# The last store of a 180-degree rotation, cut into five transfers

## The chip, the cores and the metric

The kernel runs on one core of one Trainium2 chip. The metric is the time of one execution on the device in microseconds (us); lower is better. The time before is 122.03 us, the median of three runs (121.81 to 122.38).

## The reference

```python
def setup_inputs():
    batch, c, h, w = 32, 3, 256, 256
    return {"x": np.random.randn(batch, c, h, w).astype(np.float32)}

def reference(x):
    return np.rot90(x, k=2, axes=(-2, -1)).astype(np.float32)
```

Each of the 96 images of 256 x 256 float32 values is turned by 180 degrees. Seen as one line of 65,536 values, an image comes out in reverse order. 25.17 MB are read and 25.17 MB written; there is no arithmetic.

## The kernel before

The 96 images are cut into three groups of G = 32. An image is cut into four rows of E = 16,384 values (64 KiB), so that a group fills a tile of 128 partitions with 64 KiB in each: partition 4n + s holds quarter s of image n. The three groups have tiles of their own, A, Bt and Ct; a smaller tile T of 2,048 values a partition serves as a buffer.

The work has three steps for each tile:

- **Load.** `load` (L56) brings A and Bt in one transfer each. Ct comes in three, through `rows` (L72): the even partitions, then partitions 1, 5, 9 and so on, then 3, 7, 11 and so on.
- **Turn in place.** `turn` calls `swap`, which reverses each partition's row: a piece from the back is copied reversed into T, the matching piece from the front is copied reversed to the back, and T is copied to the front. All copies are on VectorE and have the line L44. A and Ct are turned in 4 pieces of 2,048 columns, Bt in 6 of up to 1,366. The first piece of a tile takes in the first and the last columns, the last piece the middle ones. The copies keep the order in which they are written.
- **Store.** `store` (L59) writes a tile in one transfer; `[:, ::-1]` on the output's side puts quarter s in the place of quarter 3 - s, which completes the reversal of the image.

All DMAs, loads and stores, are issued by SP on one queue. The first store is tied by hand to the last copy of Bt, and the last copy but one of Bt to the second load of Ct (`after`), so that stores start when the loads are nearly in. The last store follows when Ct has been turned. Line L122 is the end of the program, where SP waits for all transfers and then for the other engines.

Of the kernel before, what the change touches and what calls it, by code (L numbers as in the profile page):

```python
# [2 lines left out]

os.environ.setdefault("NEURON_RT_ULTRASERVER_MODE", "4")

# [4 lines left out]


@with_exitstack
def kernel(
    ctx: ExitStack,
    tc: tile.TileContext,
    x: bass.AP,
    out: bass.AP,
):
    nc = tc.nc  # L20
    P = 128

    B, C, H, W = x.shape
    L = H * W
    G = 32
    E = L // 4
    J = E // 8

    x4 = x.rearrange("b c h w -> (b c) (h w)").rearrange(
        "(g n) (s e) -> g (n s) e", n=G, s=4)  # L30
    o4 = out.rearrange("b c h w -> (b c) (h w)").rearrange(
        "(g n) (s e) -> g n s e", n=G, s=4)

    pool = ctx.enter_context(tc.tile_pool(name="slots", bufs=1))
    A = pool.tile([P, E], x.dtype, tag="A")
    Bt = pool.tile([P, E], x.dtype, tag="B")
    Ct = pool.tile([P, E], x.dtype, tag="C")
    T = pool.tile([P, J], x.dtype, tag="T")

    def back(t, lo, hi):  # L40
        return t[:, hi - 1:(lo - 1 if lo else None):-1]

    def copy(dst, src):
        c = nc.vector.tensor_copy(out=dst, in_=src)  # L44
        tc.keep_in_program_order(c)
        return c

    def after(later, earlier, why):
        tc.add_manual_dep(
            later.ins, earlier.ins.name,  # L50
            mybir.DependencyInfo(
                mybir.DependencyClass.Sync, mybir.DependencyReason.DATA),
            reason=why)

    def load(t, g, lo, hi):
        return nc.sync.dma_start(out=t[:, lo:hi], in_=x4[g][:, lo:hi])  # L56

    def store(t, g, lo, hi):
        return nc.sync.dma_start(  # L59
            out=o4[g][:, ::-1, lo:hi], in_=t[:, lo:hi])  # L60

    def swap(t, lo, w):
        hi = E - lo - w
        return [
            copy(T[:, 0:w], back(t, hi, hi + w)),
            copy(t[:, hi:hi + w], back(t, lo, lo + w)),
            copy(t[:, lo:lo + w], T[:, 0:w])]

    half = E // 2

    def rows(first, step):
        return nc.sync.dma_start(  # L72
            out=Ct[first::step, :], in_=x4[2][first::step, :])

    load(A, 0, 0, E)
    load(Bt, 1, 0, E)
    rows(0, 2)
    ahead = rows(1, 4)
    rows(3, 4)

    def turn(t, pieces):
        done = []
        step = -(-half // pieces)
        for lo in range(0, half, step):
            done += swap(t, lo, min(step, half - lo))
        return done

    turn(A, 4)
    *_, last_but_one, last = turn(Bt, 6)
    after(last_but_one, ahead,  # L90
          "this copy starts when all loads but two rows are in")
    first = store(A, 0, 0, E)
    after(first, last, "the first store goes two copies after that")
    store(Bt, 1, 0, E)
    turn(Ct, 4)
    store(Ct, 2, 0, E)


# [1 line left out]
_INS = ['x']  # L100
_OUTS = [((32, 3, 256, 256), 'float32')]


# [23 lines left out]
```

## Time and profile before

| what | value |
|---|---|
| median of three runs | 122.03 us (121.81 to 122.38) |
| the profiled execution's own time | 122.06 us |
| its span, first to last instruction | 120.3 us |
| VectorE busy | 45.2 us (38%), 42 copies |
| the data queue's packets, as a share of 16 DMA engines | 97.3% |
| bytes moved, mean rate over the span | 50.33 MB, 418 GB/s |
| issue to landing: A, Bt (loads) | 22.0 us, 40.9 us |
| issue to landing: A, Bt, Ct (stores) | 22.3 us, 40.9 us, 42.7 us |
| granted TensorE clock | 1.00 (TensorE is not used) |

A page of the profile tells the busy time of each engine, the DMA queues with their packets, who waited for whom, and each DMA's time from issue to landing. A transfer is cut into packets, which 16 DMA engines carry; behind the data of a transfer each engine that served it sends a packet of 4 bytes, the completion, which counts up a semaphore. The trace holds start, duration and size of each packet, but not the number of the DMA engine that carried it. An engine can be followed through the trace since its next packet starts 3 to 4 ns before the end of the one ahead.

### The profile page before, as it was taken

How to read it: one execution, taken by the hardware profiler on the slowest of the kernel's cores; microseconds unless marked ns; L12 is line 12 of the kernel's file. 1: busy time of each engine (PE TensorE's matmuls, PEld its weight loads, DVE VectorE, ACT ScalarE, POOL GpSimd, SP SyncE). 2: the span in 40 equal slices, each digit the busy share in tenths (PEclk: the TensorE clock that was granted, in tenths of full speed). 3: DMA queues.
4: the chain of work that ended last, by engine and by line, in shares of the span. 5: the costliest groups of instructions: out<-in, count | busy, mean ns of one | idle time of the engine just before them, and what ended most of it. 6: DMA issues, size and time to landing. Idle time of an engine off the chain costs nothing.

```text
span 120.3 us, 101 instructions
## 1 busy us (share of the span) xinstructions
DVE 45.2 (38%) x42; POOL 0.2 (0%) x4
## 2 busy tenths in 40 slices
DVE  0000000499995099999459999400000000000000
POOL 0000000000000000000000000000000000000000
DMA  9889998899889988998899889988998889888980
GB/s 349 349 349 392 588 414 349 371 610 414 349 349 610 436 349 349 567 479 349 349 501 545 349 349 414 632 349 349 392 654 349 349 349 697 349 349 349 676 371 0
DMA packets 897, 50.33 MB, mean 418 GB/s; under 512 B 129, under 2 KB 129, under 8 KB 129
## 3 DMA queue, kind: packets, MB, share of 16 engines
q1 hardware_dynamic: 896, 50.33, 97.3%
q14 instruction: 1, 0.00, 0.0%
HBM read 25.17 MB, written 25.17 MB: 418 GB/s over the span
## 4 chain that ended last, share of the span: by engine, by line
DMA 34%; DVE 26%; another core or an unknown queue 2%; issue 1%; SPq 0%; DVEq 0%
DMA Bt<-in_x_dram 34%; DVE Bt L44 9%; DVE T L44 9%; DVE Ct L44 8%; SPq L56 0%; DVEq L44 0%
## 5 line engine op out<-in xcount | busy, mean ns | idle before, releaser
L44 DVE COPY T<-A 128x2048 f32<-128x2048 f32 x4 | 4.9, 1227 | 22.9 <-DMA A<-in_x_dram 22.8
L44 DVE COPY T<-Bt 128x1366 f32<-128x1366 f32 (+1 forms) x6 | 5.2, 874 | 4.5 <-DMA Bt<-in_x_dram 4.3
L44 DVE COPY T<-Ct 128x2048 f32<-128x2048 f32 x4 | 4.9, 1227 | 3.2 <-DMA Ct<-in_x_dram 3.1
L44 DVE COPY Bt<-T 128x1366 f32<-128x1366 f32 (+1 forms) x6 | 5.2, 872 | 0.2
L44 DVE COPY Bt<-Bt 128x1366 f32<-128x1366 f32 (+1 forms) x6 | 5.2, 872 | 0.2
L44 DVE COPY Ct<-T 128x2048 f32<-128x2048 f32 x4 | 4.9, 1227 | 0.1
L44 DVE COPY A<-A 128x2048 f32<-128x2048 f32 x4 | 4.9, 1227 | 0.1
L44 DVE COPY A<-T 128x2048 f32<-128x2048 f32 x4 | 4.9, 1227 | 0.1
L44 DVE COPY Ct<-Ct 128x2048 f32<-128x2048 f32 x4 | 4.9, 1227 | 0.1
L111 POOL MEMSET const-bfloat16-1.0<- 128x1 bf16 x1 | 0.1, 101 | 0.0
L111 POOL MEMSET const-uint8-127<- 128x1 uint8 x1 | 0.1, 101 | 0.0
L111 POOL MEMSET const-float32-0.0<- 128x1 f32 x1 | 0.1, 98 | 0.2 <-issue 0.2
L111 POOL MEMSET const-float32-1.0<- 128x1 f32 x1 | 0.1, 98 | 0.0
## 6 DMA issues: line engine op xcount, KB each, us to landing
Ct<-in_x_dram SPq DMA_DIRECT2D x3, 54.4
A<-in_x_dram SPq DMA_DIRECT2D x1, 22.0
Bt<-in_x_dram SPq DMA_DIRECT2D x1, 40.9
out_dram<-A SPq DMA_DIRECT2D x1, 22.3
out_dram<-Bt SPq DMA_DIRECT2D x1, 40.9
out_dram<-Ct SPq DMA_DIRECT2D x1, 42.7
```

Source lines behind the costliest of these rows:

```text
L44: c = nc.vector.tensor_copy(out=dst, in_=src)
L111: nc = _bacc.Bacc("TRN2", target_bir_lowering=False, num_devices=1)
```

## The change

The last store, of tile Ct, is issued as five transfers in place of one:

1. of the partitions 3, 7, 11 and so on (the output's quarter 0 of each image), the first 320 columns (1,280 B) for images 0 to 24: 25 rows,
2. the same for images 25 to 31: 7 rows,
3. all even partitions, full rows: 64 rows,
4. the partitions 1, 5, 9 and so on, full rows: 32 rows,
5. the partitions 3, 7, 11 and so on, columns 320 to 16,383: 32 rows of 64,256 B.

Loads, copies, and the stores of A and Bt stay as they are.

```diff
+    def store_split(t, g, w):
+        n = 0
+        for k in (25, 7):
+            nc.sync.dma_start(
+                out=o4[g][n:n + k, 0, 0:w],
+                in_=t[4 * n + 3:4 * (n + k):4, 0:w])
+            n += k
+        nc.sync.dma_start(out=o4[g][:, 3::-2, :], in_=t[0::2, :])
+        nc.sync.dma_start(out=o4[g][:, 2, :], in_=t[1::4, :])
+        nc.sync.dma_start(out=o4[g][:, 0, w:E], in_=t[3::4, w:E])
+
...
     turn(Ct, 4)
-    store(Ct, 2, 0, E)
+    store_split(Ct, 2, 320)
```

## The prediction

> **What bounds the kernel now.** I read the page first (busy shares, then the DMA part), then the DMA queue's waits, then the last stretch in windows, then the single packets.
>
> ```profile
> DVE 45.2 (38%) x42; POOL 0.2 (0%) x4
> ...
> DMA packets 897, 50.33 MB, mean 418 GB/s; under 512 B 129, under 2 KB 129, under 8 KB 129
> ...
> q1 hardware_dynamic: 896, 50.33, 97.3%
> ```
>
> VectorE works 38% of the span; the 16 DMA engines together are busy 97.3% of it. The queue's 896 packets are 768 of 65,536 B, 48 for each engine, and 128 of 4 B, the completions of 8 transfers on 16 engines. A big packet takes 2.42 us (27.1 GB/s), and on each engine one starts 3 to 4 ns before the end of the one ahead. The first starts at 1.74 us and the last ends at 119.12, so between these two nothing but DMA bytes per engine sets the time.
>
> ```profile
> SPq L59 <- DVE Bt L44: 35.7, 1, 35.7
> SPq L122 <- DMA out_dram<-Ct: 19.3, 1, 19.3
> SPq L59 <- DMA A<-in_x_dram: 19.3, 1, 19.3
> SPq L122 <- DMA out_dram<-Bt: 19.3, 1, 19.3
> SPq L59 <- DVE Ct L44: 15.2, 1, 15.2
> ```
>
> These are waits of SP, the engine that issues every DMA. The line at L59 for Ct (15.2) ends when the last copy of Ct is done, at 76.7 us. The store then issued queues behind store Bt, whose completions start at 99.5. That is 22 us of cover: VectorE and the issue are not on the path. The last wait (L122, Ct, 19.3) ends at 119.48 with the landing of the last store. From there to the end of the span, 0.80 us, is closing work.
>
> ```profile
> 116.00:116.25 0.25, 0.00 (x0) 0.00 (x0) 1.00 1.21 524
> 116.25:116.50 0.25, 0.00 (x0) 0.00 (x0) 1.00 4.24 1835
> 116.50:116.75 0.25, 0.00 (x0) 0.00 (x0) 1.00 4.24 1835
> 116.75:119.13 2.38, 0.00 (x0) 0.00 (x0) 1.00 0.00 0
> ```
>
> The last column is GB/s, put down where a packet starts: 524 in 0.25 us is 2 packets of 65,536 B, 1835 is 7. So the 16 last packets start spread out, and end from 118.59 to 119.12, with a mean of 118.88. The kernel ends with the latest engine, and perfect levelling could give 0.24 us. Packet by packet, the five engines that begin the first load earliest (1.74 to 1.81) are the five that end earliest (118.59 to 118.81); the sixth and seventh to begin end at 118.84 and 119.07, and the latest of the other nine at 119.12.
>
> **The change, part by part.**
>
> *Bytes per engine.* The last store writes the same bytes. Its last transfer (32 rows, two for each engine) is shorter by 1,280 B a row: each engine sheds 2,560 B, at 2.42 us for 65,536 B that is 0.095 us. The 32 pieces come back as transfers of 25 and 7 rows. No row of the trace shows a transfer whose rows do not divide by 16. All those in it (128, 64, 32 rows) gave every engine that served them equally many rows; if that holds, 25 rows go to five engines, five each (or to one), and 7 rows to seven engines, one each (or to one). I take five and seven, and the engines that begin first, since the split has a use only then; both are open, and are rivals below. So engines 1 to 5 get six pieces, 6 and 7 one, the other nine none.
>
> *A piece of 1,280 B.* By bytes it is 0.047 us. The smallest data-queue packet, the 4-byte one, shows 9 ns, so with it 0.056 us: the low end. The high end comes from the nearest odd rows, the 8,192 B instruction packets on the other queue: 0.32 to 0.53 us where bytes make 0.30, so up to 0.23 us above bytes, 0.28 us a piece. I take 0.056: the store packets stand back to back, as these pieces will, while those instruction packets stood alone before the span. Below bytes it cannot come; the big packets show no faster rate.
>
> *Completions.* Store Ct goes from one transfer to five. Engines 1 to 5 get four more 4-byte packets, 6 and 7 three, the others two. From the end of one big packet to the start of the next is -3 ns without a completion and +2 to +3 ns with one: 6 ns each, 0.024, 0.018 and 0.012 us.
>
> *End of the data.* Engines 1 to 5: 118.81 - 0.095 + 6 x 0.056 + 0.024 = 119.08. Engines 6 and 7: 119.07 - 0.095 + 0.056 + 0.018 = 119.05. The other nine: 119.12 - 0.095 + 0.012 = 119.04. Latest 119.08 against 119.12: a gain of 0.04 us.
>
> *Order of the rows.* The even rows, then every fourth, in place of all 128. Loads of Ct already go in this pattern and land 9.67, 4.85 and 4.84 us apart, 19.36 together; the load of Bt took 19.35. Store packets now average 2.423 us and load packets 2.420. By the pattern I cost nothing; were the eight last packets as quick or slow as the extremes of the steady rows (2.418 and 2.432), it would be -0.04 or +0.07 us.
>
> *Issues and waits.* The program as built lets the 25-row transfer wait for the third copy of Ct only, since that copy writes the columns 0 to 319 last. So SP issues 25 and 7 rows at about 65.4 us, and then waits for the last copy, as now. The even rows go out at 76.7 and the last two after them, 0.54 to 0.60 us each (rows L59 and L72), done by 78.6. The queue works in order on each engine (landings now come strictly in order of issue), so nothing moves before 99.5, and the cover is 21 us; without it four more issues would cost 2.4 us. Behind SP's new waits stand only its own later stores. No engine waits for the first two.
>
> *The closing waits.* The built program keeps eight completion counters. With 12 transfers in place of 8, four counters are used twice, and the last transfer lands on that of the second Ct load. SP's four closing waits test two counters each, in an order that does not change, and that counter is in the first. Now three of them pass before the last store lands (at 77.3, 80.8 and 100.1) and only the fourth waits for it; after the change the first waits for it, and the other three, long satisfied, stand behind it. In the trace one such wait, from its start to the next instruction, is 119.482 to 119.550, 0.068 us. Three: +0.20 us, with no cover. From below: nothing, if satisfied waits pass at once; from above, three times the 0.1 us that separate some of the barrier's steps behind.
>
> **Sum.** -0.04 + 0.20 = +0.16 us on the profiled execution, which had a span of 120.28 and a time of 122.06 (1.78 outside the span, unchanged): 122.22. The median of the three runs shown is 0.03 below it, so 122.2. This is +0.13%; a measurement of this kernel can tell about 0.5%, 0.61 us, from no change.
>
> **Rivals.**
> *Dear pieces (slower).* Place: engines 1 to 5, behind store Bt, at about 99.5 us. A piece at 0.28 us makes 118.81 - 0.095 + 6 x 0.28 + 0.024 = 120.42, 1.30 later, with the closing waits 123.56. It decides over 0.5% from 0.13 us a piece (119.53 = 118.74 + 6 x 0.13). For it: the first packet of each engine, at 2.86 to 3.65 us, shows what work outside a stream can cost. Against: the 3 ns overlap of neighbours. Chance 0.11.
> *All on one engine.* 32 x 0.056 = 1.79 us on a single engine, ending 1.19 to 1.72 us later: 123.5 to 124.0. Rows of the trace neither exclude nor show it. Chance 0.03.
> The Trainium skill (DMA: Bandwidth & Descriptors, section on why a DMA increments its semaphore by 16) says that the engines used are the largest number up to 16 that divides both sides' slowest dimension, the lowest-numbered first: 25 rows on five, 7 on seven. By that rule this rival falls and the sum stands; no row here can show it.
> *Each transfer pays its landing.* If an engine held back until a transfer's completion had landed (118.59 to 118.96 now for the first: 0.37 us), four more would cost engines 1 to 5 1.5 us, less the 0.3 by which they were early, with the closing waits: 123.4. Against it: on each engine the next transfer's first packet starts 3 ns before the completion packet ends, with no gap. Chance 0.03.
> The same page (section on the anatomy of one DMA) gives each transfer a fixed 2.0 us, most of it waiting for the receipt; four more, one behind the other, would make 130 us. The trace disagrees, as the three loads of Ct show with 19.36 us.
> *The early engines are not those served (the change does not do what it says).* If the latest of all is among the five: 119.12 - 0.095 + 0.336 + 0.024 = 119.39, with the waits +0.47: 122.5. Chance 0.13; a third of that, with pieces a little dearer, passes 0.5%.
> *Closing waits free.* -0.04: 122.0, chance 0.10.
> *Faster by over 0.5%.* Even perfect levelling is 0.24 us; only a faster packet rate would do it, and none of the 768 is below 2.418 us. Chance 0.03.
>
> **How the numbers follow.** Forecast 0.57; with free waits and two thirds of the unserved case, within 0.5%: 0.57 + 0.10 + 0.09 = 0.76. Slower: 0.11 + 0.03 + 0.03 + 0.04 = 0.21. Faster 0.03. The range goes from 121.85 (free waits, the quick rows' -0.04, 0.1 of spread between medians) to 122.95 (a piece of about 0.18 us), leaving out some 0.15 above and 0.04 below.
>
> **What would show it.** Right: 12 x 16 - 20 = 172 completions of 4 B and 32 packets of 1,280 B; their duration near 0.056 us; last data end near 119.08; four closing waits close together after the last landing, and 1.0 us instead of 0.80 from the landing to the end. Wrong: pieces of over 0.13 us, 25 of them on one chain, gaps behind completions, or a steady packet off 2.42 us.

## The result, and the profile after

The changed kernel takes 122.47 us (median of 7 runs, 122.43 to 122.69), the kernel before 122.01 (7 runs, 121.81 to 122.38). The ratio is 1.0039 with a 95% interval of 1.0026 to 1.0053: about 0.46 us slower (0.32 to 0.65), inside the range of the forecast (122.2, from 121.85 to 122.95) and within the 0.5% that was called no change. The changed kernel's profiled execution took 122.46 us, with a span of 120.67.

From the page after, the same three lines as were read before:

```profile
DVE 45.2 (37%) x42; POOL 0.2 (0%) x4
...
DMA packets 972, 50.33 MB, mean 417 GB/s; under 512 B 172, under 2 KB 204, under 8 KB 204
...
q1 hardware_dynamic: 972, 50.33, 97.1%
```

172 completions, and 204 - 172 = 32 packets under 2 KB, the pieces: as forecast. The other 768 are 736 of 65,536 B and 32 of 64,256 B. VectorE has not moved. SP's waits (engine, line, what it waited for, us in all, times, longest):

```profile
SPq L133 <- DMA out_dram<-Ct: 39.7, 1, 39.7
...
SPq L69 <- DVE Ct L44: 9.1, 1, 9.1
SPq L65 <- DVE Ct L44: 3.9, 1, 3.9
```

The two small transfers go out after a wait on VectorE of 3.9 us at L65, the even rows after another 9.1 us at L69: these two stand in place of the 15.2 us of before. At the end there is one wait of 39.7 us, where before the waits for stores A, Bt and Ct came one after the other: the first closing wait now holds the last store's counter. The trace has it from 80.037 to 119.699 us, and behind it three more at 119.741, 119.808 and 119.873.

The windows over the last packets of the changed kernel (last column: GB/s of the packets that start in the stretch):

```profile
116.00:116.25 0.25, 0.00 (x0) 0.00 (x0) 1.00 0.59 257
116.25:116.50 0.25, 0.00 (x0) 0.00 (x0) 1.00 3.56 1542
116.50:116.75 0.25, 0.00 (x0) 0.00 (x0) 1.00 4.16 1799
116.75:117.00 0.25, 0.00 (x0) 0.00 (x0) 1.00 1.19 514
```

At 64,256 B a packet these are 1, 6, 7 and 2. Before, none started after 116.75. The spread between engines has grown, not shrunk.

The 0.40 us between the two profiled executions have two parts. The last data are the end of the last packet of rows; a landing is the last step of a completion counter.

| execution | last data of store Bt | last data of all | from the one to the other | last landing | from it to the span's end |
|---|---|---|---|---|---|
| before | 99.757 | 119.124 | 19.367 | 119.466 | 0.81 |
| after | 99.742 | 119.350 | 19.608 | 119.677 | 0.99 |

0.18 us are closing work, and 0.24 us are data behind store Bt. (Store Bt ended 0.015 us earlier in the execution after, and the landing came 0.015 us closer behind the data, which is why the two add up to slightly more than 0.40.)

### The profile page after: what moved, and what is told of

It reads as the page before. It is cut to its first block, busy times and chain, and to the rows that moved or that the text cites. A ratio compares the mean times of both kernels' runs of the same rounds, so it can differ in the third digit from the quotient of the medians.

```text
span 120.7 us, 105 instructions
## 1 busy us (share of the span) xinstructions
DVE 45.2 (37%) x42; POOL 0.2 (0%) x4
## 4 chain that ended last, share of the span: by engine, by line
DMA 34%; DVE 25%; another core or an unknown queue 2%; issue 1%; SPq 0%; DVEq 0%
DMA Bt<-in_x_dram 34%; DVE Bt L44 9%; DVE T L44 9%; DVE Ct L44 8%; SPq L56 0%; DVEq L44 0%
```

## The experiments

All times are against the kernel before on the same chip and day. Differences are of medians; ratios and their intervals are of means, so the two need not agree in the last digit. Two columns of the table above are given with most runs, since they are free of what happened ahead of the last store: "end" is the time from the last landing to the span's end, "data" the time from the last data of store Bt to the last data of all. One profiled execution stands behind each of these. In the six profiles with equal bytes for each engine or with pieces of 256 B, "data" lies between 19.31 and 19.41.

**1. The closing waits alone, and the pieces alone.** Stores A and Bt are cut into four and two transfers, all of rows that divide by 16. That moves the last store's counter into the first closing wait of the kernel before (12 transfers), and into the last one of the changed kernel (16).

```diff
-    first = store(A, 0, 0, E)
+    def quarter(t, g, s):
+        return nc.sync.dma_start(out=o4[g][:, 3 - s, :], in_=t[s::4, :])
+
+    first = quarter(A, 0, 0)
...
-    store(Bt, 1, 0, E)
+    for s in (1, 2, 3):
+        quarter(A, 0, s)
+    nc.sync.dma_start(out=o4[1][:, 3::-2, :], in_=Bt[0::2, :])
+    nc.sync.dma_start(out=o4[1][:, 2::-2, :], in_=Bt[1::2, :])
```

> The kernel before, with store A as four transfers of 32 rows and store Bt as two of 64: 12 transfers, so that the last store's counter falls in the first of SP's four closing waits, as in the changed kernel; the last store itself is one transfer of 128 rows. Theory (closing waits cost 0.20 us, the pieces on the five served engines cost the rest): +0.20 us against before, four closing waits together after the last landing, the last data end where it was (119.12 give or take 0.1). Rival (the closing waits only look dear, the time is in the data): within 0.05 us of before.

Measured +0.14 us (1.0013, interval 1.0005 to 1.0022). From the last landing to the span's end 0.99 us, the data behind store Bt 19.373. The closing wait stands out in the waits of this kernel:

```profile
SPq L128 <- DMA out_dram<-Ct: 42.2, 1, 42.2
```

> The changed kernel with the same cut of stores A and Bt: 16 transfers, the last store's counter falls in the last closing wait again. Theory: 0.20 us below the changed kernel, about +0.25 us against before, since the pieces stay. Rival (all of the loss is closing work): equal to before.

Measured +0.29 us (1.0020, 1.0009 to 1.0030): end 0.82 us again, data 19.558. SP's closing wait falls apart into four again, as before the change:

```profile
SPq L139 <- DMA out_dram<-Ct: 39.4, 4, 20.4
```

The theory holds in both: the closing waits and the data are separate prices, 0.14 and 0.29, and their sum, 0.43, is the change's 0.46 but for the measurement's width.

**2. Light pieces.** `store_split(Ct, 2, 64)`, with 12 transfers and then with 16.

> The changed kernel with pieces of 64 columns (256 B) in place of 320. Theory (the five served engines are not the early ones, and their load sets the end): a piece is about 0.018 us, the served engines gain 0.11 + 0.02 - 0.02 us in place of 0.27, so the end comes some 0.15 us sooner than in the changed kernel: +0.3 us against before. Rival (the odd transfers cost by their number, whatever they carry): as the changed kernel, +0.46. Rival (the forecast's: the served engines are early, the others set the end and are now relieved less): 0.08 us later than the changed kernel, +0.54.

Measured +0.21 us (1.0017, 1.0009 to 1.0026): end 1.00, data 19.382. Both rivals are out; the theory's +0.3 lies at the upper end of the interval (0.11 to 0.32 us). Of 32 pieces 31 show 0.018 us. The pieces label the engines here: the five that carry six of them ended store Bt at 99.360, 99.408, 99.442, 99.507 and 99.565, places 2, 4, 6, 8 (or 9, two end together) and 11 of 16 in order of ending. The latest (99.800) was none of them.

> Pieces of 256 B and 16 transfers: both prices taken away at once, the five transfers of the last store kept. If closing waits and the load of the served engines are all, it equals before within 0.1 us; if five transfers cost something else, it stays 0.15 us or more above.

Measured +0.01 us (1.0001, 0.9992 to 1.0010): 121.96 against 121.95. With both prices taken away the five transfers cost nothing, and bring nothing either. This shows that the price in the data goes with the bytes of the pieces on the engines they serve; it does not tell how.

**3. Five transfers without odd rows.** First with transfers that take images 0 to 15 and 16 to 31 apart:

```diff
+    def store_split(t, g, w):
+        for n in (0, 16):
+            nc.sync.dma_start(
+                out=o4[g][n:n + 16, 3::-2, :], in_=t[4 * n:4 * n + 64:2, :])
+        nc.sync.dma_start(out=o4[g][:, 2, :], in_=t[1::4, :])
+        for n in (0, 16):
+            nc.sync.dma_start(
+                out=o4[g][n:n + 16, 0, :], in_=t[4 * n + 3:4 * n + 64:4, :])
...
-    store(Ct, 2, 0, E)
+    store_split(Ct, 2, 320)
```

> The last store in five transfers whose rows all divide by 16 (even rows of images 0 to 15 and 16 to 31, then partitions 1, 5, 9 and so on, then 3, 7, 11 and so on for images 0 to 15 and 16 to 31): each engine gets the same eight packets of 65,536 B as before. Theory: closing waits alone, +0.20 us, data end moved by no more than the completions' 0.02. Rival (cutting the store or its row order costs in the data): +0.4 us or more.

Measured 136.21 us, +14.29 (ratio 1.1173, 1.1148 to 1.1197). Neither theory had this. The transfer of 32 rows over all partitions took its usual time (123.0 to 124.9 us at the landings, behind 120.0); the others, whose 16 engines all read from one half of the partitions, took about twice theirs: the second landed 10.3 us behind the first. Two kernels tell cutting from halves apart: one with a transfer for each quarter of the image over all partitions and the last quarter in two halves of its columns, and one that only cuts the last store of the kernel before into partitions 0 to 63 and 64 to 127.

> The last store in five transfers of 32 rows over all 128 partitions (one for each quarter, the last quarter in two halves of its columns): no odd piece, equal bytes for each engine, 12 transfers. Theory (closing waits cost 0.13 to 0.20 us, cutting by itself nothing; the 14 us of the five equal transfers came from reading 64 of the 128 partitions): +0.15 to +0.20 us. Rival (cutting the store in five costs by itself): +10 us or more, as there.

Measured +0.18 us (1.0016, 1.0004 to 1.0027): end 0.99, data 19.383. Five transfers cost their closing waits and nothing else.

> The kernel before with its last store in two transfers, partitions 0 to 63 and 64 to 127: full rows, 64 rows each, nine transfers. Theory (16 engines that read the same 64 partitions get about half their rate: in the five equal transfers 32 rows from one half took 9 to 10 us where 4.84 is usual): the last store takes up to twice its 19.35 us, +15 to +19 us. Rival (it was the small number of rows or the strides there): within 0.1 us of before.

Measured 142.61 us, the median of two runs, +20.64 (1.1692, 1.1670 to 1.1715). The windows show it, with store Bt in the first line and the two halves in the others:

```profile
82.00:98.00 16.00, 0.00 (x0) 0.00 (x0) 1.00 1.07 459
102.00:118.00 16.00, 0.00 (x0) 0.00 (x0) 1.00 0.95 197
122.00:136.00 14.00, 0.00 (x0) 0.00 (x0) 1.00 1.04 220
```

The column before the last is the busy share of the DMA engines: they are as busy, at half the bytes (459 GB/s, then 197 and 220). The longest packets took 5.3 us. One thing stays open: in both slow kernels a transfer from half of the partitions also writes only half of the group's images, one half of its 8.39 MB of output. No run has the one without the other, so that it is argued, but not shown, that reading from half of the partitions is the cause.

**4. Where the odd transfers lose their time.** In the changed kernel's packet records 27 of the 32 pieces took 0.055 us, and five took 0.095, 0.099, 0.120, 0.168 and 0.224. Followed along the engines, two of the five served engines (those with six pieces) needed about 0.55 and 0.70 us for them and their completions, the other three 0.32 to 0.39. (The two and an engine without pieces end store Bt within 3 ns, so that it is not certain which is which.) One of the two also stood idle for 0.22 us between two pieces, from 99.513 to 99.732. That made two theories: A, the hold-ups; and B, the plain load of an engine that is late already. First the pieces on all engines, in one transfer:

```diff
-        for k in (25, 7):
-            ...
+        nc.sync.dma_start(out=o4[g][:, 0, 0:w], in_=t[3::4, 0:w])
```

> The 32 pieces of 1,280 B go in one transfer of 32 rows in place of 25 and 7, so all 16 engines get two pieces each, from the partitions of which they also carry the full rows; 11 transfers, so two closing waits stand behind the last landing. Theory (in the changed kernel two of the five served engines were held up for 0.2 to 0.4 us at their pieces, since these come from partitions that other engines are reading at the time): no piece much over 0.055 us, data end moved by +0.02, closing +0.13: +0.15 us against before. Rival (a piece is dear wherever it comes from, 0.1 us and more): +0.25 us or more. Rival (the load of the five engines alone, without hold-ups, makes the loss): +0.15 us, but then pieces_last stays at +0.46.

Measured +0.17 us (1.0008, 0.9998 to 1.0019): end 0.93 (two waits behind), data 19.414. All 32 pieces took 0.055 us. Two on each of 16 engines are not dear. Then the two small transfers behind the large ones:

> The changed kernel with the 25 and 7 rows issued behind the three large transfers; the same packets for each engine, 12 transfers, three closing waits behind the last landing. Theory (hold-ups from partitions that others read): the early engines' pieces run beside the others' last full packets, the late ones' alone, so hold-ups shrink where they count: +0.25 to +0.40 us against before. Rival (the load of the five engines alone): the same bytes on the same engines, +0.46 us as in the changed kernel.

Measured +0.57 us (1.0046, 1.0031 to 1.0060), where the theory of hold-ups forecast 0.25 to 0.40, which only touches the lower end of the interval (0.38 to 0.73). No piece was held up, all took 0.055 us, and the time stayed. Once more, with a second profile:

> The changed kernel with the 25 and 7 rows last, once more, for a second profile: the pieces were 0.055 us each without a hold-up, and the time was +0.56. Theory B: from the last landing of store Bt to the last landing of all some 0.1 to 0.2 us more than the 19.36 us of before, time +0.35 to +0.5. Rival (a small transfer at the end lands later behind its data, 0.4 to 0.56 us where full rows take 0.35): the same data end as theory B, and 0.1 to 0.2 us on top, +0.5 to +0.6.

Measured +0.53 us (1.0045, 1.0032 to 1.0057). In the two profiles the data behind store Bt took 19.300 and 19.258 us, 0.07 and 0.11 *less* than before: here the levelling works. But the last landing came 0.55 and 0.45 us behind the last completion packet, 0.34 in the kernel before, and the end cost 0.99 us. These make +0.32 and +0.18; in both profiles store Bt ended late, too, at 99.90 and 99.96. Whether that is chance stays open, and with it 0.25 to 0.35 us of this kernel. So its time is no proof for theory B: it stayed, but not by way of the data.

The changed kernel once more:

> The changed kernel once more, for a second profile. Theory A (held-up pieces): again two or more of the five served engines are held up for 0.2 us and more at their pieces, and one of these ends last. Theory B (the five served engines stand anywhere in the order, and 0.33 us of pieces on a late one sets the end): the five engines hold places spread over the sixteen by the end of store Bt, and the last to end is a served one, held up or not. Time +0.46 us in both.

Measured +0.54 us (1.0042, 1.0030 to 1.0054): end 1.00, data 19.576. One served engine was clearly held up (0.221 and 0.098 us for two pieces), but it was the one that had ended store Bt first of all, at 99.198, so it cost nothing. The last to end was a served engine without a hold-up: it ended store Bt at 99.782, 2 ns before the latest of all, and began its next full row at 100.126, 0.344 later. The profile of after_16_transfers says the same: the latest of all at the end of store Bt (99.983) was a served one, and began its next row 0.324 later. Theory B holds in these two. In the first profile of the changed kernel theory A does: the last to end was one of the two held up, from place 6, 7 or 8, while the five served engines stood early, at places 1, 3, 10 and two of 6 to 8. Then three times the bytes:

> The changed kernel with pieces of 960 columns (3,840 B). Theory B: a piece takes about 0.146 us in place of 0.052, six of them 0.56 us more, while each engine sheds 0.19 us more in the last rows: +0.37 us on the changed kernel, +0.83 against before. Theory A (hold-ups, which come with each odd piece and not with its bytes): +0.27 us or less above the changed kernel's data end less 0.19, so +0.3 to +0.5 against before. The forecast's picture (served engines early by 0.3 us): +0.5.

Measured +1.88 us (1.0132, 1.0104 to 1.0160, or 1.27 to 1.95 us), more than any theory said. Theory A's bound and the forecast's picture are out, and B's +0.83 falls short as well. The profiled run does not help: it took 122.64 us, the fastest of six (123.43 to 123.89 the others); in it 31 of 32 pieces took 0.149 us, and the five served engines stood at place 7 or before. What happens in the others was not seen; that hold-ups grow with the bytes is a guess.

## Why the prediction was right, and where it was not

**The closing waits: right.** Forecast +0.20 us for three satisfied waits behind the last landing; 0.18 in the profile, +0.14 and +0.18 as times (12 transfers with nothing else changed, and five even transfers). It follows from the completion counters, as the built program shows them, and undoing that alone gives it back.

**Issues, cover, order of rows, completions: right.** SP issued 25 and 7 rows at 65.2 and 66.1 us and the rest from 76.6. Here the issues were dearer than the 0.54 to 0.60 us taken: five took 0.87, 1.26, 0.60, 1.38 and 1.36 us. The last is done at 80.0 in place of 78.6, against 99.3, when the first engine has ended store Bt (99.2 in the kernel before, where the forecast wrote 99.5); the cover holds. Rows by quarters cost nothing (five even transfers: data 19.383 against 19.367).

**Five and seven engines: right.** The counters tell it: that of the 25 rows rose at once at 66.45 us and then in five landings from 99.88 to 100.40, that of the 7 rows in seven. Here is the row that the forecast lacked for the rule of the Trainium skill (DMA: Bandwidth & Descriptors, section on why a DMA increments its semaphore by 16) by which 25 rows go to five engines and 7 rows to seven, and it agrees. That those are the lowest-numbered engines the trace cannot show.

**Which engines, and what six pieces cost them: wrong.** The step that failed is the end of the data. It let the five served engines end store Bt first, 0.3 us ahead of the latest, gave each 0.36 us for six pieces and their completions, and came out at -0.04 us; measured is +0.24. The two halves of that step failed in different executions.

In the profile of the changed kernel the places were nearly as forecast: the last of the five to end store Bt did so at 99.512, 0.23 us ahead of the latest engine. The latest engine that was not held up ended 19.343 us behind store Bt, 0.02 less than before. What failed there is the price: two of the five took 0.55 and 0.70 us in place of 0.36, and the slower one ended last.

In the profiles of after_16_transfers and changed_again the places failed: a served engine ended store Bt last of all, or 2 ns from it. On an engine that is late already the sum of the forecast gives 0.27 us more, and 6 x 0.052 + 0.02 - 0.095 = 0.24 with the pieces' measured spacing; these two profiles have 0.19 and 0.21. This is the rival "the early engines are not those served", 122.5 with a chance of 0.13. That its figure was met so closely is in part luck, since the first profile has its 0.24 by the other road. The range of the forecast held because it was wide enough for this rival; of the two terms of its sum, -0.04 and +0.20, only the second came.

The forecast took five early engines out of one profile and put the five served ones in their place, with the reason that the split has a use only then. In the five profiles in which the served engines can be told, they lean to the early side: 23 of their 25 places are among the first eleven of 16. But the forecast needed all five early in every execution, and one late one is enough to set the end. In the profile before, moreover, the link from the first to begin to the first to end leads through 60.3 to 60.9 us, between the last load and the first store. There about ten engines pause for 0.03 to 0.13 us, and none of these can be followed with certainty.

**A piece: right in most, with a tail.** Forecast as 0.056 us, it took 0.055, 27 times of 32; the other five took up to 0.224. The dear pieces of the rival (0.28 for each) did not come, the worst engine needing 0.70 us for six. Nor did one engine for all, nor a landing paid by each transfer: behind the completion of one small transfer the piece of the next starts 3 to 4 ns before the completion's end. (The 2.0 us that the forecast sets beside this last rival stand, in the section of the Trainium skill that it names, for DMAs issued through GpSimd; here SP issues them.)

## What to carry to other kernels

Levelling a stream of DMAs by giving some engines more bytes needs to know which engines are early in *every* run, and what the extra packets cost when they are held up; one profile shows only that some engines are early. Here even perfect levelling had 0.24 us to give, and the extra transfers alone cost 0.14 to 0.18 us at the program's end, since the counter of the last one was waited for first: count the transfers, and see on which counter the last one falls. And cut a large store by rows that cover all partitions, as the five even transfers do; cut into partitions 0 to 63 and 64 to 127, the same bytes took twice as long.

## What the runs showed of the hardware that was not expected

- 16 DMA engines that all read from 64 of the 128 partitions, and write half of the group's output: 197 and 220 GB/s where the store of 128 partitions makes 459 in the same execution; +20.64 us for one store of 8.39 MB.
- In the two profiles that end with the small transfers, the last landing comes 0.45 and 0.55 us behind the last completion packet, against 0.32 to 0.35 in the kernels that end with larger rows (32 KiB and more).
- Pieces of 1,280 B, six on each of five engines, one on each of two, and ahead of the large transfers, are sometimes held up (0.06 to 0.24 us in place of 0.055, for five, six and eight of 32 in three profiles). Two on each of 16 engines were not (0 of 32 in one profile), and behind the large transfers only 0 and 2 of 32 were. Why was not settled; the trace does not tell which engine reads which partition.
- SP needs 1.23 to 1.55 us for many of the smaller store issues of these kernels, those that follow right behind others (0.54 to 0.64 for those of 128 rows, 0.49 to 0.60 for most smaller ones that come first behind a wait). It counts only where nothing covers it.
